# Out-projection left to the scheduler, every group of the up-projection with two token pairs

## The chip, the cores and the metric

The kernel runs on one core of one Trainium2 chip. The metric is the device time of one execution in microseconds (us): the median of several runs. Five kinds of work appear in the profile: TensorE matmuls (PE) and its weight loads (PEld), VectorE (DVE), ScalarE (ACT), GpSimd (POOL) and the DMA engines. SyncE (SP) and POOL issue the DMAs. Each engine takes its instructions in one order, fixed when the program is built.

## The reference

One step of a one-layer streaming encoder, for 2048 new tokens and 64 tokens of a running stream. After a mixer (a recurrent branch and an attention branch, added to `mixed`) comes a feed-forward block with a width-3 causal convolution over the tokens:

```python
x = x + mixed @ w_out                       # 1024 -> 1024
xn2 = rmsnorm(x, norm_ffn)
up = xn2 @ w_up                             # 1024 -> 5632
up_c = causal_dwconv(up, ...)               # three taps per channel
gate, val = split(up_c)
x = x + (silu(gate) * val) @ w_down         # 2816 -> 1024
y = rmsnorm(x, norm_final)
```

All is float32. The kernel splits each matmul operand into a high and a low part and adds three products (high by high, high by low, low by high).

## The kernel before

The 2112 tokens form three **pairs** of column blocks (`PAIRS`): pairs 0 and 1 have 2 x 304 columns each, pair 2 has 2 x 448. The kernel has four stages after one another: the mixer with its projections (stage 1, up to line 734), the out-projection (`wout`, lines 852 to 871), the up-projection (the loop over `plan`, lines 1408 to 1516) and the down-projection (the loop over `seq`, from line 1577).

**Order.** In stage 1 the tile framework's scheduler orders the instructions of each engine: it simulates the core and, among the instructions that are ready in its simulation, takes the one that stands first in the program. From line 739 on (`tc.manual_schedule()`) the order on each engine is the order in which the Python program states the instructions. So the interleaving of stages two to four is written out by hand: generators such as `mixes`, `xprep`, `xsums` and `xread` are driven a few pieces at a time between the matmuls (`drive`), and dictionaries `later` and `then` hold work that is due in a given step.

**Out-projection.** For each pair `i` and each of 8 row blocks `m`, two half weights (`weights[j]`) are multiplied with the pair's two blocks, 24 matmuls for each half weight. In pair 0 the weights come raw from `w_out` and are split (`wsplit`), and a POOL DMA stores the split form in `woS` (line 398); in pairs 1 and 2 `wload` (line 390) reads them back on SP, 512 KB each. Beside this run: loads of `mixS` and their splits into the operands of the next pair (`mixes`, lines 363 to 372), the residual (line 875) with its loads of `xT` (line 849) and stores of `x1S` (line 876) on POOL, and `xprep`, which prepares the operands of the up-projection of pairs 0 and 1 from `x1S` (loads on line 799, scaling on line 811, splits by `put2`). Three of pair 1's seven operands (`x1`, line 1389) are made in the up-projection's first four steps, in a region `FA` that takes the place of an out-projection operand region `RC`.

**Up-projection.** A group `g` is one of 22 row blocks of `w_up` with its partner 22 blocks on; groups `f` and `f + 11` follow one another. The two-by-two block product of a group with a pair is done with seven products in place of eight (Winograd's scheme), one product a step: `ORDER` names the seven token operands, `wops` makes the seven weight operands. A **lane** is one group with one pair; a product in a lane is 12 matmuls. `Lane.product` issues them, `Lane.after` takes the sums out of PSUM: in steps 0, 1, 2 and 6 on ACT (lines 1137, 1150), in steps 3, 4 and 5 on DVE (lines 1141, 1143, 1148). Then follow the convolution (`conv_a` on ACT, line 1122; `conv_b` on DVE, line 1128), the gate (lines 1153, 1162) and sums that are stored in `hS`.

`steps` gives the order: 20 groups with pairs 0 and 1 together (two lanes that share a weight, 140 steps); then groups 10 and 21 with pair 0 alone and after that with pair 1 alone (28 steps with one lane); then all groups with pair 2, two groups at a time (77 steps). With pair 0 alone done, `give(0)` frees all seven operands of pair 0 at once, and `xread` starts to read pair 2's operands into the space: 28 reads of 224 KB from `xS`, each rounded on ACT and subtracted on DVE, with 5 buffers. `give(1)` frees pair 1 when its last step is done.

**Weights.** A weight operand is a combination of raw blocks (DVE, `comb`, line 934), rounded to its high part (ACT, line 205, in `split2`) and subtracted to the low part (DVE, line 206, a step later, through the list `plow`). The first time (`fresh`) four of seven are stored in `wuS` for pair 2. `prepare` does this in the step's middle, after the products are issued and ahead of `Lane.after`; there are 4 weight slots. Groups 10 and 21 get theirs from `wsums`, which makes them in halves beside the first steps, with two slots `wx`; their one-lane steps read them from `wuS` (line 930), and split three of seven again, for either pair.

**Beside the up-projection.** `fill` drives one piece a step: first `wsums` for groups 10 and 21, then `xsums`, which makes pair 2's operands in float32 and stores them in `xS` (96 pieces).

**Down-projection.** 33 steps for each of seven products; beside them `side` does residuals, squares, the last norm (`rms`, line 752, whose sum over channels is a matmul) and the outputs (line 1571), two pieces a step from product 4 on. The last product ends with pair 0, `(i, p) == (6, 0)`, in 33 small steps.

Of the kernel before, what the change touches and what calls it, by code (L numbers as in the profile page):

```python
# [7 lines left out]
F32 = mybir.dt.float32  # L8
# [6 lines left out]
P = 128  # L15
# [3 lines left out]
NF = 22  # L19
# [107 lines left out]
def kernel(ctx: ExitStack, tc: tile.TileContext, xT, w_in, w_out, w_up, w_dn, gw, pk,  # L127
# [609 lines left out]

    es2 = ExitStack()
    es2.enter_context(tc.manual_schedule())
# [38 lines left out]
    def give(p):  # L778
        for region, part in xparts.pop(p):
            region.taken.remove(part)  # L780
# [132 lines left out]
    plow = []  # L913

    def wops(g, fresh):
# [3 lines left out]
        def parts(src):  # L919
            t = wh.tile([P, 2, 4 * P], F32R, name="wh")  # L920
            plow.append(split2(t[:, 0], t[:, 1], src))
            return t

        def kept_s(i, src):
            t = wh.tile([P, 2, 4 * P], F32R, name="wh")
            if fresh:
                low = split2(t[:, 0], t[:, 1], src())
                plow.append(lambda: (low(), nc.gpsimd.dma_start(wuS[g, i], t.bitcast(F32))))
            else:
                nc.sync.dma_start(t.bitcast(F32), wuS[g, i])  # L930
# [20 lines left out]

    def wsums(g, pool, out):

        for h in range(2):
            def draw(o, name):
                t = pool.tile([P, 2 * P], F32, name=name)
                c = 4 * P * (o[1] == "2") + h * 2 * P
                nc.sync.dma_start(t, w_up[g + NF * (o[0] == "2")][:, c:c + 2 * P])
                return t

            low = []

            def keep(i, src):
                t = out.tile([P, 2, 2 * P], F32R, name="wx", bufs=2)
                f = split2(t[:, 0], t[:, 1], src)
                low.append(lambda: (f(), nc.gpsimd.dma_start(wuS[g, i][:, :, h * 2 * P:(h + 1) * 2 * P],
                                                             t.bitcast(F32))))

            a, b, c, d = draw("11", "wa"), draw("21", "wb"), draw("22", "wc"), draw("12", "wd")
            for _ in range(4):  # L970
                yield
            nc.vector.tensor_tensor(a, a, b, op=ALU.subtract)
            keep(0, a)
            yield
            low.pop(0)()
            nc.vector.tensor_tensor(a, c, a, op=ALU.subtract)
            keep(1, a)
            yield
            low.pop(0)()
            nc.vector.tensor_tensor(b, b, c, op=ALU.add)  # L980
            keep(2, b)
            yield
            low.pop(0)()
# [796 lines left out]
```

## Time and profile before

| what | value |
|---|---|
| runs shown | 3041.38 us median of 3 (3038.78 to 3042.38) |
| profiled execution, its own time | 3043.69 us |
| its span, first to last instruction | 3041.9 us |
| matmuls | 17640, PE busy 2886.8 us |
| DVE busy | 2064.7 us (68%) |
| ACT busy | 1541.4 us (51%) |
| POOL busy | 450.5 us (15%) |
| HBM traffic | 195 GB/s over the span |

Busy time of PE overstates its work, because matmuls overlap one another. A better measure is the distance from the start of one matmul to the start of the next: where nothing is waited for it is constant, and a stretch's length less its matmuls times that distance is what the stretch loses. A window counts the instructions that touch it, so it counts about two matmuls too many.

### The profile page before, as it was taken

The numbers are of one execution on the slowest core, as the hardware profiler recorded it, in microseconds if no ns is written. First come the engines' busy times: TensorE is split into PE (matmuls) and PEld (weight loads), VectorE is DVE, ScalarE is ACT, GpSimd is POOL, SyncE is SP. The second block draws the span as 40 slices with busy tenths as digits, with TensorE's granted clock in tenths as the row PEclk, the third lists the DMA queues.
The fourth block names the chain that finished last, engine by engine and source line by source line (L and its number), as shares of the span: only waits on it lengthen the run. The fifth ranks groups of instructions, "written<-read, shape, count | busy, mean of one in ns | idle before, by whom it ended". The sixth has DMA issues, their size and how long they took to land. (4 is left out here: it accounts for less than half of the span.)

```text
span 3041.9 us, 48860 instructions
## 1 busy us (share of the span) xinstructions
PE 2886.8 (95%) x17640; PEld 2764.9 (91%) x17640; DVE 2064.7 (68%) x4048; ACT 1541.4 (51%) x3426; POOL 450.5 (15%) x655
## 2 busy tenths in 40 slices
PE   8999999999999999998797999999899999999998
PEld 7989889999998999997797999999799998999997
DVE  5388783477775378774656888888666656656676
ACT  4577772476672476673323555554544444433432
POOL 3232112000000000004120333333000101000001
PEclk9999999999999999998898999999999999999999
DMA  7776547534336544328774656566866666977563
GB/s 246 262 237 196 181 153 243 178 128 136 124 118 205 184 137 144 119 84 287 241 237 146 216 210 219 205 220 220 314 209 215 208 218 190 273 219 217 157 213 118
DMA packets 324499, 595.37 MB, mean 196 GB/s; under 512 B 37168, under 2 KB 224544, under 8 KB 307360
## 3 DMA queue, kind: packets, MB, share of 16 engines
q1 hardware_dynamic: 285728, 461.45, 47.4%
q0 software_dynamic: 38528, 130.79, 11.6%
q8 instruction: 139, 2.28, 0.3%
q14 instruction: 104, 0.85, 0.1%
HBM read 400.99 MB, written 191.64 MB: 195 GB/s over the span
## 5 line engine op out<-in xcount | busy, mean ns | idle before, releaser
L230 PE MATMUL mm<-xh,whl 128*128 128x320 f32 (+2 forms) x2112 | 692.3, 328 | 10.0 <-ACT xh L200 5.2
L231 PE MATMUL mm<-xl,whl 128*128 128x320 f32 (+2 forms) x2112 | 689.4, 327 | 7.6 <-POOL xl L201 3.8
L232 PE MATMUL mm<-xh,whl 128*128 128x320 f32 (+2 forms) x2112 | 688.2, 326 | 1.4 <-POOL whl L201 1.4
L205 ACT ACTIVATE RE<-FW 128x512 fp32r<-128x512 f32 (+3 forms) x556 | 296.8, 554 | 475.1 <-DVE FW L934 114.9
L230 PEld LDWEIGHTS mm<-xh,whl 128*128 128x128 f32 x2112 | 403.5, 191 | 17.0 <-ACT xh L200 8.1
L231 PEld LDWEIGHTS mm<-xl,whl 128*128 128x128 f32 x2112 | 403.1, 191 | 15.9 <-POOL xl L201 6.4
L232 PEld LDWEIGHTS mm<-xh,whl 128*128 128x128 f32 x2112 | 402.6, 191 | 2.4 <-POOL whl L201 1.7
L206 DVE TENSOR_TENSOR RE<-FW,RE 128x512 fp32r<-128x512 f32 (+3 forms) x556 | 319.9, 596 | 104.4 <-ACT RE L205 103.5
L1128 DVE SCALAR_TENSOR_TENSOR FA<-FA,pkt 128x608 f32<-128x608 f32 (+1 forms) x264 | 245.9, 951 | 71.6 <-ACT FA L1122 67.0
L1092 PE MATMUL mf<-RA,RE 128*128 128x304 f32 (+1 forms) x608 | 201.4, 331 | 10.6 <-ACT FW L1137 8.2
L1591 PE MATMUL mf<-RE 128*128 128x304 f32 (+2 forms) x616 | 198.9, 323 | 7.1 <-ACT RE L205 4.7
L1094 PE MATMUL mf<-RA,RE 128*128 128x304 f32 (+1 forms) x608 | 199.6, 328 | 4.8 <-DVE RE L206 4.8
L1592 PE MATMUL mf<-RE 128*128 128x304 f32 (+2 forms) x616 | 199.0, 323 | 0.2 <-DVE RE L206 0.2
L1093 PE MATMUL mf<-RA,RE 128*128 128x304 f32 (+1 forms) x608 | 199.0, 327 | 0.0
L1593 PE MATMUL mf<-RE 128*128 128x304 f32 (+2 forms) x616 | 197.8, 321 | 0.0
L1122 ACT ACTIVATE FA<-FA,pkt 128x608 f32<-128x608 f32 (+1 forms) x132 | 128.4, 973 | 110.4 <-DVE FA L1143 104.2
L1092 PE MATMUL mf<-RE 128*128 128x304 f32 (+1 forms) x488 | 159.9, 328 | 12.9 <-ACT RE L205 9.6
L1093 PE MATMUL mf<-RE 128*128 128x304 f32 (+1 forms) x488 | 159.9, 328 | 1.6 <-DVE RE L206 1.6
L1094 PE MATMUL mf<-RE 128*128 128x304 f32 (+1 forms) x488 | 159.9, 328 | 0.0
L201 POOL TENSOR_TENSOR gl<-gr,gh 128x256 fp32r<-128x256 f32 x24 | 22.4, 932 | 789.0 <-ACT gh L200 789.0
L1092 PEld LDWEIGHTS mf<-RA,RE 128*128 128x128 f32 x608 | 115.3, 190 | 18.9 <-ACT FW L1137 11.8
L1092 PE MATMUL mm<-RE 128*128 128x304 f32 (+1 forms) x392 | 125.4, 320 | 7.2 <-ACT FW L1137 4.4
(331 smaller groups left out, 7132.4 us busy)
## 6 DMA issues: line engine op xcount, KB each, us to landing
whl<-wiS SPq DMA_DIRECT2D x88, 1024.0 KB, 5.1
RE<-wuS SPq DMA_DIRECT2D x104, 512.0 KB, 4.5
wiS<-whl SPq DMA_DIRECT2D x44, 1024.0 KB, 4.8
wuS<-RE POOLq DMA_DIRECT2D x80, 512.0 KB, 3.8
FW<-in_w_up_dram SPq DMA_DIRECT2D x158, 256.0 KB, 5.1
hS<-FA POOLq DMA_DIRECT2D x154, 152.0 KB, 3.9
FW<-hS SPq DMA_DIRECT2D x154, 152.0 KB, 3.5
FW<-in_w_in_dram SPq DMA_DIRECT2D x44, 512.0 KB, 5.8
```

What stands on the lines that cost most here:

```text
L205: nc.scalar.activation(hi, src, AF.Copy)
L206: return lambda: nc.vector.tensor_tensor(lo, src, hi.bitcast(F32), op=ALU.subtract)
L230: nc.tensor.matmul(ps[:, :n], wh[:, c], xh[:, k, :n], start=first, stop=False)
L231: nc.tensor.matmul(ps[:, :n], wh[:, c], xl[:, k, :n], start=False, stop=False)
L232: nc.tensor.matmul(ps[:, :n], wl[:, c], xh[:, k, :n], start=False, stop=last)
L1092: nc.tensor.matmul(ps[:, :n], w[:, 0, c], x[:, k, 0], start=first, stop=False, **more)
L1093: nc.tensor.matmul(ps[:, :n], w[:, 0, c], x[:, k, 1], start=False, stop=False, **more)
L1094: nc.tensor.matmul(ps[:, :n], w[:, 1, c], x[:, k, 0], start=False, stop=last, **more)
L1128: nc.vector.scalar_tensor_tensor(uc, G[:, j:j + self.cols], col("fw", 44 * j + m), uc, op0=ALU.mult, op1=ALU.add)
L1591: nc.tensor.matmul(ps[m][:, cs], w[:, 0, c], t[:, 0], start=k == 0, stop=False)
L1592: nc.tensor.matmul(ps[m][:, cs], w[:, 0, c], t[:, 1], start=False, stop=False)
L1593: nc.tensor.matmul(ps[m][:, cs], w[:, 1, c], t[:, 0], start=False, stop=k == 10)
```

## The change

All 22 groups run with pairs 0 and 1 together (154 steps), so the one-lane steps, `wsums` and the slots `wx` go, and there are 5 weight slots. In the last group's seven steps (`last` is its first step) `give(p, u)` frees operand `u` of pairs 0 and 1 as soon as its product has been issued, and `xread` puts pair 2's operands there, up to three reads a step, with 3 buffers in the first steps and 5 after; `free` says in which step room for one more operand of pair 2 is open. `xsums` advances in three steps of four. The manual order is entered behind the out-projection, at the up-projection's loop; the out-projection, with the first three weights and with `xprep` as far as it runs there, is ordered by the scheduler. The rounding of weights (`phigh`) is held back until `rounded()`, behind `Lane.after`. In the down-projection the last pair drives one side piece a step in place of two.

```diff
--- before.py
+++ after.py
@@ -734,9 +734,7 @@
     es1.close()
 
 
-
     es2 = ExitStack()
-    es2.enter_context(tc.manual_schedule())
     pff = es2.enter_context(tc.tile_pool(name="pff", bufs=5, space=PSUM))
     bank = [0]
 
@@ -775,9 +773,9 @@
         xparts.setdefault(p, []).append((region, part))
         xops[p, o] = region.view(part, [P, 4, 2, n])
 
-    def give(p):
-        for region, part in xparts.pop(p):
-            region.taken.remove(part)
+    def give(p, q):
+        region, part = xparts[p][q]
+        region.taken.remove(part)
 
     def put2(p, o, k, src):
         return split2(xops[p, o][:, k, 0], xops[p, o][:, k, 1], src)
@@ -910,7 +908,11 @@
         nc.sync.dma_start(t, w_up[m][:, c:c + 4 * P])
         return t
 
-    plow = []
+    phigh, plow = [], []
+
+    def rounded():
+        while phigh:
+            phigh.pop(0)()
 
     def wops(g, fresh):
 
@@ -918,14 +920,18 @@
 
         def parts(src):
             t = wh.tile([P, 2, 4 * P], F32R, name="wh")
-            plow.append(split2(t[:, 0], t[:, 1], src))
+            phigh.append(lambda: plow.append(split2(t[:, 0], t[:, 1], src)))
             return t
+
+        def keep(i, t, src):
+            low = split2(t[:, 0], t[:, 1], src)
+            plow.append(lambda: (low(), nc.gpsimd.dma_start(wuS[g, i], t.bitcast(F32))))
 
         def kept_s(i, src):
             t = wh.tile([P, 2, 4 * P], F32R, name="wh")
             if fresh:
-                low = split2(t[:, 0], t[:, 1], src())
-                plow.append(lambda: (low(), nc.gpsimd.dma_start(wuS[g, i], t.bitcast(F32))))
+                src = src()
+                phigh.append(lambda: keep(i, t, src))
             else:
                 nc.sync.dma_start(t.bitcast(F32), wuS[g, i])
             return t
@@ -948,44 +954,6 @@
         yield kept_s(2, lambda: comb("21", "21", "22", ALU.add))
         yield parts(r["12"])
         yield kept_s(3, lambda: comb("12", "12", "11", ALU.subtract))
-
-    def wsums(g, pool, out):
...
     def xsums(p, pool, rpool, width):
 
@@ -1027,15 +995,15 @@
                 for _ in range(2):
                     yield
 
-    def xread(p, names, pool):
+    def xread(p, names, pools):
 
         n, raw = PAIRS[p][0][1], []
         todo = [(o, k) for o in names for k in range(4)]
         low = None
         for j, (o, k) in enumerate(todo):
-            while len(raw) < min(j + 4, len(todo)):
+            while len(raw) < min(j + len(pools[-1].slots["xs"]) - 1, len(todo)):
                 oo, kk = todo[len(raw)]
-                raw.append(pool.tile([P, n], F32, name="xs", bufs=5))
+                raw.append(pools[-1].tile([P, n], F32, name="xs"))
                 nc.sync.dma_start(raw[-1], xS[ORDER.index(oo), kk])
             if k == 0:
                 operand(p, o)
@@ -1067,11 +1035,10 @@
     class Lane:
 
 
-        def __init__(self, g, p, lanes):
-
-            self.g, self.p, self.steps = g, p, (1, 2, 3, 3) if p == 2 else (1, 4, 3, 4)
-            if len(lanes) == 1:
-                self.steps = (1, 2, 2, 2) if p == 1 and g == 21 else (1, 5, 5, 6)
+        def __init__(self, g, p):
+
+            self.g, self.p = g, p
+            self.steps = (1, 2, 3, 3, 4) if p == 2 else (1, 2, 2, 2, 2) if g == 21 else (1, 4, 3, 4, 5)
             (self.t0, self.n), (self.t1, _) = PAIRS[p]
             self.cols = 2 * self.n + (2 if self.t1 + self.n > TP else 0)
 
@@ -1178,7 +1145,7 @@
             def sums_c():
                 nc.vector.tensor_tensor(h[:, :n], h[:, :n], self.e[:, :n], op=ALU.subtract)
 
-            s, a, b, c = self.steps
+            s, a, b, c, d = self.steps
             if g < 11:
                 at(s, lambda: store("11", h[:, :n]))
                 at(a, sums_a)
@@ -1188,15 +1155,12 @@
                 at(b, sums_b)
                 at(c, sums_c)
                 at(c, lambda: (store("T2", self.e[:, :n]), store("T3", self.e[:, n:])))
-                at(c if p == 1 and s == a - 1 == c - 1 else c + 1, lambda: store("T4", h[:, :n]))
+                at(d, lambda: store("T4", h[:, :n]))
 
     def steps():
-        forder = [f + o for f in range(11) for o in (0, 11)]
-        for f in forder[:20]:
-            yield [(f, 0), (f, 1)], True
-        for p in (0, 1):
-            for f in forder[20:]:
-                yield [(f, p)], False
+        for f in range(11):
+            for g in (f, f + 11):
+                yield [(g, 0), (g, 1)], True
         for f in range(11):
             yield [(f, 2), (f + 11, 2)], False
 
@@ -1358,9 +1322,8 @@
                 tp.close()
                 wr.reserve("wr", 4 * P, 4)
                 wh.close()
-                wh.reserve("wh", 8 * P, 4)
+                wh.reserve("wh", 8 * P, 5)
                 wh.turn["wh"] = 2
-                wh.reserve("wx", 4 * P, 2)
                 prime(0)
                 prime(0)
             work = wout(i, m, besides if i == 0 or m > 0 else lambda: drive(side, pace[0] if i == 1 else 0))
@@ -1369,6 +1332,7 @@
             if i == 2 and m == 7:
                 for made in (0, 1, 2):
                     prepare(made)
+                    rounded()
                 made = 3
         residual(i, 7, work)
         drive(side, 99)
@@ -1396,41 +1360,39 @@
 
     lane_sums(BS)
     up["c"].reserve("G", 2 * BS + 2, 3)
+
+    es2.enter_context(tc.manual_schedule())
     fill, x2, raw2 = [], [], [0]
 
 
-    live, extra = [], [10, 21]
+    live = []
 
     def fits(i):
         return sum(len({g for g, _ in plan[q][0]}) for q in range(i, min(made + 1, len(plan)))) <= len(wh.slots["wh"])
 
+
+    last, free = 21 * 7, (1, 1, 2, 2, 4, 4, 5)
     px = rx = None
     for i, (lanes, fresh, u) in enumerate(plan):
         if u == 0:
-            live = [Lane(g, p, lanes) for g, p in lanes]
-            if lanes == [(10, 0)]:
-
-                assert not extra
-                wh.close("wx")
-                wh.extend("wh", 8 * P, 1)
-            if lanes == [(10, 1)]:
-
-                drive(fill, 999)
-                px.close()
-                rx.close()
-                give(0)
+            live = [Lane(g, p) for g, p in lanes]
+            if i == last:
+                xs = [Pool(FW, FA)]
+                xs[0].reserve("xs", BM, 3)
+                x2 = [xread(2, ORDER, xs)]
+            if i == last + 7:
                 RD.close()
                 FP = Region(tc, "FP", 9728, F32, "right")
-                px = Pool(FP)
-                x2 = [xread(2, ORDER, px)]
-            if lanes == [(0, 2), (11, 2)]:
-                assert raw2[0] <= 17
-                drive(x2, 17 - raw2[0])
-                give(1)
+                xs.append(Pool(FP))
+                xs[1].reserve("xs", BM, 5)
                 up["s"].close()
                 up["s"] = Pool(FW)
-                lane_sums(BM)
+                for name in ("p1", "p7"):
+                    up["s"].reserve(name, BM, 2)
                 wh.extend("wh", 8 * P, 4)
+        if i == last + 9:
+            xs[0].close()
+            up["s"].reserve("V", BM, 2)
         clock[0] = i
         for f in later.pop(i, ()):
             f()
@@ -1443,6 +1405,9 @@
             up["u"].reserve("uc", 2 * BM + 2, 4)
         for lane in live:
             lane.product(u, ready[i, lane.g])
+        if last <= i < last + 7:
+            give(0, u)
+            give(1, u)
         while made < len(plan) + 1 and fits(i):
             prepare(made)
             made += 1
@@ -1450,6 +1415,7 @@
             f()
         for lane in live:
             lane.after(u)
+        rounded()
         if i < 4:
             drive(x1, 5)
             if i == 0:
@@ -1472,25 +1438,24 @@
             lane_sums(BS)
             up["h"].reserve("hp", 2 * BS, 4)
             px, rx = Pool(FW), Pool(FA)
-        if i > 6 and not fill:
-            if extra:
-                px.close()
-                fill = [wsums(extra.pop(0), px, wh)]
-            elif px.regions[0] is FW and lanes != [(10, 1)] and lanes[0][1] == 0 and not raw2[0]:
-                px.close()
-                fill = [xsums(2, px, rx, BM // 2)]
-                raw2[0] = 1
-        drive(fill, 1)
-        if x2:
-            if lanes[0][1] == 1:
-                for _ in range(2):
-                    if raw2[0] < 17:
-                        drive(x2, 1)
-                        raw2[0] += 1
-            else:
-                drive(x2, 99 if u == 3 else 3)
-                if u == 3:
-                    px.close()
+        if i == 7:
+            fill = [xsums(2, px, rx, BM // 2)]
+        if i % 4 != 3:
+            drive(fill, 1)
+        if i == last - 1:
+            drive(fill, 999)
+            px.close()
+            rx.close()
+        if last < i < last + 11:
+
+            q = sum(i - last >= f for f in free)
+            for _ in range(3):
+                if raw2[0] < 4 * q:
+                    drive(x2, 1)
+                    raw2[0] += 1
+            if i == last + 10:
+                drive(x2, 99)
+                xs[1].close()
         if lanes[0] == (0, 2) and u == 4:
             up["h"].reserve("hp", 2 * BM, 2)
 
@@ -1514,7 +1479,8 @@
             dloads(0, 10)
             tparts(0)
             tparts(1)
-    give(2)
+    for q in range(7):
+        give(2, q)
     wh.extend("wh", 8 * P, 6)
     dr.extend("hh", 2 * BM, 5)
 
@@ -1605,7 +1571,7 @@
                 tparts(len(seq) - 36 + k)
             if k < 6:
                 raw[6, 0, k - 2] = dtoken("T4", 0, k - 2)
-        drive(side, 3 if R is None else 1 if i < 4 else 2)
+        drive(side, 3 if R is None else 1 if i < 4 or (i, p) == (6, 0) else 2)
         if j == 8:
 
             drive(side, 99)
```

## The prediction on record

> **What bounds the kernel now.** I read the page first (busy times, slices), then the windows by stage, then for each stage with a loss the waits of PE, and behind these the waits of the engine that PE waited for.
>
> ```profile
> span 3041.9 us, 48860 instructions
> PE 2886.8 (95%) x17640; PEld 2764.9 (91%) x17640; DVE 2064.7 (68%) x4048; ACT 1541.4 (51%) x3426; POOL 450.5 (15%) x655
> PE   8999999999999999998797999999899999999998
> ```
>
> PE is busy nearly throughout; slices 20, 22 and 29 show 7, 7 and 8. The question is what PE loses where. The windows give it (us, then busy time and count for PE, PEld, DVE, ACT, POOL; granted clock, DMA share, GB/s):
>
> ```profile
> 700.00:1300.00 600.00, 589.05 (x3628) 572.52 (x3627) 413.18 (x979) 362.26 (x802) 15.17 (x17) 0.99 0.45 146
> 1956.00:1996.00 40.00, 40.00 (x289) 40.00 (x288) 33.48 (x61) 18.96 (x46) 13.91 (x26) 1.00 0.64 214
> 2190.00:2540.00 350.00, 350.00 (x1695) 317.92 (x1694) 210.24 (x308) 156.25 (x388) 37.60 (x70) 1.00 0.66 220
> 1371.77:1521.82 150.05, 120.99 (x773) 118.18 (x773) 82.62 (x173) 48.42 (x107) 44.38 (x76) 0.88 0.79 268
> 1521.82:1602.01 80.19, 80.19 (x390) 72.85 (x389) 45.99 (x86) 18.79 (x38) 20.16 (x37) 1.00 0.69 229
> 1602.01:1647.64 45.63, 27.89 (x149) 25.33 (x148) 32.04 (x55) 14.74 (x34) 3.77 (x7) 0.74 0.48 156
> 1647.64:2110.26 462.62, 453.81 (x3218) 449.01 (x3217) 393.72 (x683) 238.67 (x568) 150.25 (x276) 1.00 0.60 209
> 2110.26:2175.39 65.13, 50.62 (x338) 48.60 (x337) 43.47 (x74) 33.65 (x77) 10.69 (x20) 0.97 0.86 289
> 2998.00:3020.40 22.40, 17.84 (x123) 15.88 (x121) 20.84 (x36) 8.39 (x20) 4.56 (x9) 1.00 0.32 111
> ```
>
> Rows two and three hold no loss: two edge matmuls taken off, a 304-column matmul starts every 40/287 = 0.1394 us, a 448-column one every 350/1693 = 0.2067 us. A two-lane step (24) is 3.35 us, a one-lane step 1.67 us, a pair 2 step 4.96 us. With the counts from the code:
>
> - Out-projection, pairs 0 and 1 (row four): 768 matmuls are 107.1 us of 150.05; lost 43.0. Pair 2 (row five): 384 are 79.4 of 80.19; lost 0.8.
> - First six up-projection steps (row six): 144 are 20.1 of 45.63; lost 25.6.
> - The other two-lane steps (row seven): 3216 are 448.3 of 462.62; lost 14.3.
> - One-lane steps (row eight): 336 are 46.8 of 65.13; lost 18.3.
> - Pair 2 (row three): nothing.
>
> About 102 us are lost in a quarter of the span, and the change touches nearly each of these places. The matmuls stay the same in number and shape: one-lane steps load weights for each matmul just as two-lane steps do.
>
> **Part 1: the out-projection in the scheduler's order.** PE's waits from 1371.77 to 1602.01, and some of SP's there (total, times, longest):
>
> ```profile
> PE mf L863 <- DMA RE<-woS: 11.5, 3, 7.7
> PE mm L863 <- DMA RE<-woS: 6.8, 1, 6.8
> PE mf L865 <- DVE RA L206: 4.4, 3, 1.9
> PE mm L865 <- DVE RA L206: 4.0, 2, 2.7
> PE mm L863 <- ACT RA L205: 3.6, 1, 3.6
> PE mf L863 <- ACT RA L205: 2.4, 1, 2.4
> ...
> SPq L363 <- DVE RE L206: 24.5, 6, 7.4
> SPq L390 <- PE mm L865: 21.7, 6, 5.0
> SPq L799 <- DVE FW L819: 19.7, 4, 9.0
> ...
> RE<-woS SPq DMA_DIRECT2D x32, 512.0 KB, 5.7
> ```
>
> PE waits 32.7 us in all; the other 11 of 43.8 are matmuls at a low clock after a wait (clock 0.88). Of the waits 18.3 us are late `woS` weights. They land 5.7 us after issue, and with five slots each is allowed some three steps, 10 us; late they are because SP stands at an `x1S` load (line 799) or a `mixS` load (line 363) whose buffer isn't free yet, with the `woS` load behind it. An order made by readiness puts the ready load first. So the 18.3 us go, and of the low clock their share, 11 x 18.3/32.7 = 6.2: 24 us. The RA waits (14.4) I leave: the first 6.3 are the split of pair 0 at the stage's start, which is data, and the others hang on `woS` stores in POOL's order and on transfers. What is late next are these. Ends: 38 gained (all but the first 6), or 50 lost (first rival). That readiness order can work here is row one: stage 1 is in that order, and in 600 us PE is idle for 11. But it moves 146 GB/s, and the out-projection 268.
>
> **Part 2: the first six steps.** Nothing gained.
>
> ```profile
> PE mf L1092 <- ACT RE L205: 9.6, 2, 6.9
> PE mf L1094 <- DVE RE L206: 4.1, 1, 4.1
> ...
> DVE FA L811 <- DMA FA<-x1S: 9.1, 4, 3.7
> ```
>
> PE waits for operand T1 of pair 1, four rounds of load, scale, split, subtract and split, which can't start before the out-projection's last matmul frees RC. The order is stated there before and after. The fifth slot adds a weight to step 0 (one rounding, one subtraction, 1.3 us by the durations in part 3) and takes it from a later step: 3 us either way.
>
> **Part 3: roundings last.** In row seven DVE is busy for 85%, ACT for 52%. PE's waits there, ACT's longest, and one case from the timeline:
>
> ```profile
> PE mf L1092 <- ACT FW L1137: 7.6, 10, 1.4
> ...
> ACT RE L205 <- DVE FW L934: 111.8, 51, 6.2
> ...
> 1808.46 0.68 DVE L934 TENSOR_TENSOR FW<-FW 128x512 f32<-128x512 f32 x1
> 1809.17 0.63 ACT L205 ACTIVATE RE<-FW 128x512 fp32r<-128x512 f32 x1 [1.88 <-DVE FW L934]
> 1809.70 0.72 ACT L1137 ACTIVATE FW<-mf 128x304 f32<-128x304 f32 x2
> 1810.16 0.41 PE L1092 MATMUL mf<-RA,RE 128*128 128x304 f32 x1 [1.40 <-ACT FW L1137]
> ```
>
> ACT's rounding (line 205) stands ahead of the copies out of PSUM and waits for DVE's `comb`, which queues behind convolution and `xsums`; the copies come late, and PE's next product into that bank waits. With the copies first this wait goes. Against it: the rounding now ends up to two copies and itself, 0.72 + 0.63 = 1.35 us, behind a step's end, and DVE's low part early in the next step queues `comb` and convolution behind it. DVE has 0.15 x 3.35 = 0.5 us free a step, so in some steps it will run late. The weights are needed four steps on, which hides that. Of 14.3 us I take 10; ends 0 and 14. `wsums` gone and `xsums` in three steps of four lie on DVE beside PE: no term of their own.
>
> **Part 4: no one-lane steps, operand by operand.** Waits from 2110.26 to 2178, and the reads of pair 2 there:
>
> ```profile
> PE mm L1092 <- ACT FW L1137: 7.8, 3, 3.4
> PE mf L1092 <- ACT FW L1137: 3.8, 2, 3.3
> ...
> ACT RA L205 <- DMA FP<-xS: 9.8, 6, 3.7
> ...
> L205 ACT ACTIVATE RA<-FP 128x448 fp32r<-128x448 f32 x16 | 8.8, 572 | 9.9 <-DMA FP<-xS 9.8
> FP<-xS SPq DMA_DIRECT2D x28, 224.0 KB, 5.1
> ```
>
> ACT stands 9.8 us in the one-lane steps for reads of `xS`, with PSUM copies queued behind: two reads a 1.67 us step, with five buffers. Those steps go, and their 18.3 us with them. But 18 reads now fall into six two-lane steps, three in 3.35 us, with three buffers and two reads ahead. A buffer's turn is landing (5.1; the `mixS` loads of that size took 4.7), rounding 0.57, subtraction 0.62: 6.3 us. Three buffers pass three reads in that time, where a step has 3.35. If ACT is held the whole of it, a step is 6.3: five steps (the first three reads are ahead) lose 15 us. Steps 3, 4 and 5 leave PSUM on DVE, not on ACT, the buffers' turn shortens where fewer bytes move (row eight 289 GB/s, row seven 209), and PE is a step ahead: I take 8, between 0 and 15. So 10 us gained; ends 3 and 18. Freeing operand by operand costs nothing: a space is written only after copies that waited for the same products.
>
> **Part 5: one side piece a step in the last pair.**
>
> ```profile
> PE mm L1592 <- DVE RE L206: 3.4, 4, 2.0
> PE mm L752 <- DVE FD L1558: 2.1, 2, 1.2
> PE mf L752 <- DVE FD L1558: 1.1, 1, 1.1
> ```
>
> In the last row of the windows DVE is busy for 20.84 of 22.40 us: two outputs of a side piece each stand ahead of the token's low part. Half as many a step halve PE's 6.6 us: 3 gained. One or two output pieces go behind the last matmul, about 0.5 each; ends -1 and 6.
>
> **Sum.** 24 + 0 + 10 + 10 + 3 = 47 us. The profiled execution took 3043.7 us (span 3041.9, 1.8 around it): 2996.7. It stood 2.3 over the median of the runs, so 2994.
>
> **Rivals.**
>
> *The transfers bind the out-projection.* Pairs 0 and 1 move 150.05 us x 268 GB/s = 40.2 MB. The densest stage row is 289 GB/s at a DMA share of 0.86; at that rate 40.2 MB take 139 us, whatever the order, and part 1 gains 11 in place of 24: 3007. For it: a share of 0.79 already. Against: pair 2 runs without loss at 229 GB/s. The Trainium skill, "DMA: Bandwidth & Descriptors", section Specifications, puts the HBM limit of a core at about 358 GB/s; by it the bytes would take an estimated 112 us and not bind, and part 1 could give up to 38. No row here shows such a rate over a stage.
>
> *The order does not change to the better.* The scheduler goes by the program's order among what is ready; if its simulated transfers are quicker than the real ones, it finds SP never blocked and repeats the stated order. Part 1 gives 0: 3018.
>
> *Slower.* The same fault in a worse form: by modelled times it issues `woS` loads one step ahead of use. A landing of 5.7 us against a step of 3.35 is 2.35 late, with the low clock after it (11/32.7 of a wait) 3.1; in pair 2 5.7 - 4.96 = 0.7, 1.0 with the clock. 16 steps of each: 66 us, less the 24.5 of woS waits and their clock that are there now, is 41 lost. With the other parts' 23 gained: 3041 + 18 = 3059. It decides from 23 us lost on. Every queue that the loads pass on SP bears on it; against it is row one.
>
> *Buffers.* ACT held the whole time by three buffers, 15 us: part 4 gains 3, and all else as forecast 3001.
>
> **How the numbers follow.** 0.2% (6 us) is about what a measurement here can tell from no change. Forecast, the buffers' case with it: 0.48. Transfers bind: 0.20. Order not better: 0.15. Slower: 0.12. An out-projection that loses about what the rest gains: 0.05. So faster 0.83, same 0.05, slower 0.12. Low end: parts 1, 3, 4 and 5 at their better ends add 14 + 4 + 8 + 3, part 2 3: 2994 - 32 = 2962. High end: the order rival (3018) with part 4 at its worse end (7) and part 3 at 0 (10) is 3035; above it lie the last two cases, 0.17.
>
> **What would show it.** Right: from the first out-projection matmul to the first of the up-projection about 206 us in place of 230; the six first steps at 43 to 49; the group "ACT L205 <- DVE L934" near nothing, and PE waits for L1137 in the two-lane steps under 3 us; no `wx`; in the last group's seven steps some 8 us of waits on PSUM copies behind `FW<-xS`; pair 2 without loss. Wrong: an out-projection of 230 us or more, `RE<-woS` still among PE's waits, DVE later in the two-lane steps with PE waiting for line 1141 or 1143, or a new gap where the manual order begins.

## The result, and the profile after

The changed kernel took 3001.53 us in the median (four runs, 3000.28 to 3006.32), the kernel before 3041.88 (four runs, 3038.78 to 3049.98): a ratio of 0.9866, with the interval 0.9844 to 0.9888. The forecast was 2994, in a range of 2962 to 3035. The profiled execution took 3006.32 us (span 3004.6), 37.3 less in its span than the one before; the medians differ by 40.4.

Three lines of the page, then the windows by stage (us, then busy time and count for PE, PEld, DVE, ACT, POOL; granted clock, DMA share, GB/s). Each window begins and ends with the first matmul of a stage.

```profile
span 3004.6 us, 48626 instructions
PE 2870.3 (96%) x17640; PEld 2755.8 (92%) x17640; DVE 2059.1 (69%) x4026; ACT 1544.0 (51%) x3412; POOL 444.9 (15%) x647
PE   8989999999998999998897999999899999999997
```

```profile
1373.00:1499.27 126.27, 114.01 (x772) 112.51 (x773) 78.37 (x169) 49.97 (x106) 43.03 (x74) 0.92 0.90 310
1499.27:1579.47 80.20, 80.20 (x390) 72.85 (x389) 48.28 (x94) 19.62 (x40) 20.21 (x37) 1.00 0.72 245
1579.47:1628.88 49.41, 27.72 (x150) 25.30 (x148) 31.70 (x55) 15.15 (x35) 3.78 (x7) 0.72 0.41 133
1628.88:2077.33 448.45, 448.45 (x3218) 448.45 (x3217) 384.15 (x654) 238.50 (x553) 140.54 (x262) 1.00 0.58 203
2077.33:2125.82 48.49, 47.09 (x338) 46.87 (x337) 37.61 (x64) 27.58 (x61) 10.22 (x20) 1.00 0.62 205
2125.82:2178.20 52.38, 42.44 (x194) 38.01 (x193) 35.45 (x58) 27.79 (x70) 6.42 (x12) 0.90 0.79 283
2960.87:2987.60 26.73, 25.64 (x204) 24.53 (x202) 22.05 (x39) 7.23 (x18) 6.55 (x13) 1.00 0.25 88
2987.60:3004.60 17.00, 2.02 (x7) 1.12 (x6) 9.99 (x28) 1.87 (x6) 2.58 (x5) 0.57 0.42 134
```

The counts of matmuls are those of before, so stage can be set against stage. A **half-step** is the 12 matmuls of one lane: 1.67 us with pairs 0 and 1, of which there are 308 in either kernel, and 2.48 us with pair 2. Loss is length less matmuls times their spacing, 0.1394 and 0.2067 us, as in the prediction.

| stretch | before | after | gained | forecast |
|---|---|---|---|---|
| out-projection, first matmul to first of the up-projection | 230.2 | 206.5 | 23.7 | 24 |
| first six steps, length | 45.6 | 49.4 | -3.8 | 0 |
| other steps up to half-step 280 (all two-lane), loss | 14.2 | 0.0 | 14.2 | 10 |
| half-steps 280 to 308 (one-lane before), loss | 18.3 | 1.6 | 16.7 | } 10 |
| first 16 half-steps of pair 2 (308 to 324), loss | 1.0 | 12.7 | -11.7 | } |
| down-projection up to the last matmul of its products (its last 33 steps: 32.5, 26.7) | 470.1 | 463.7 | 6.4 | } 3 |
| behind that matmul (the last norm with its own matmuls, outputs) | 10.1 | 17.0 | -6.9 | } |

With 1.2 us lost ahead of the out-projection and 0.1 in the rest of pair 2 the rows give 37.3, the difference of the spans. The two largest terms are as forecast or better. Two stretches that were to lose nothing now lose: the start of pair 2 and the tail.

What PE waits for after, in the out-projection (first fence), the first six steps (second) and around the start of pair 2 (third): total, times, longest.

```profile
PE mf L750 <- DVE FW L882: 11.1, 1, 11.1
PE mm L861 <- ACT RA L205: 4.0, 1, 4.0
PE mm L863 <- DVE RA L206: 1.2, 1, 1.2
```

```profile
PE mf L1059 <- ACT RE L205: 12.7, 2, 6.9
PE mf L1059 <- ACT FA L1104: 5.8, 1, 5.8
PE mf L1060 <- DVE RE L206: 3.1, 2, 2.5
```

```profile
PE mf L1061 <- DVE RE L206: 7.9, 1, 7.9
PE mf L1059 <- issue: 1.8, 1, 1.8
PE mf L1059 <- DVE FA L1110: 1.4, 1, 1.4
```

`RE<-woS` is gone from the out-projection's list. By the two traces five of the 32 stored weights landed 0.2 us or less ahead of their first matmul in the kernel before, and none less than 1.5 us ahead after; the shortest time from a load's issue to that matmul grew from 4.2 to 7.1 us. In its place stands one wait of 11.1 us of the norm's matmul (line 750) for a sum of squares. The timeline shows what that sum stood behind: SP's queue, then ACT's.

```profile
1430.15 20.14 SPq L363 DMA_DIRECT2D FW<-mixS  x12
...
1433.49 0.58 ACT L205 ACTIVATE RE<-FW 128x448 fp32r<-128x448 f32 x1 [8.21 <-DMA FW<-mixS]
1438.86 0.58 ACT L205 ACTIVATE RC<-FW 128x448 fp32r<-128x448 f32 x1 [3.32 <-DMA FW<-mixS]
```

Twelve `mixS` loads hold SP for 20 us, since they wait for buffers; ACT's roundings wait for the loads, with the squares of the residual behind them.

### The profile page after: what moved, and what is told of

Its sections match the earlier page's. It is cut to its first block, busy times and chain, and to the rows that moved or that the text cites. A ratio compares the mean times of both kernels' runs of the same rounds, so it can differ in the third digit from the quotient of the medians.

```text
span 3004.6 us, 48626 instructions
## 1 busy us (share of the span) xinstructions
PE 2870.3 (96%) x17640; PEld 2755.8 (92%) x17640; DVE 2059.1 (69%) x4026; ACT 1544.0 (51%) x3412; POOL 444.9 (15%) x647
## 5 line engine op out<-in xcount | busy, mean ns | idle before, releaser
L205 ACT ACTIVATE RE<-FW 128x512 fp32r<-128x512 f32 (+2 forms) x544 | 290.2, 559 | 418.4 <-DVE FW L940 101.7
L206 DVE TENSOR_TENSOR RE<-FW,RE 128x512 fp32r<-128x512 f32 (+2 forms) x544 | 315.7, 601 | 173.8 <-ACT RE L205 168.4
L1061 PE MATMUL mf<-RA,RE 128*128 128x304 f32 (+1 forms) x620 | 204.2, 329 | 7.9 <-DVE RE L206 7.9
L1059 PE MATMUL mf<-RA,RE 128*128 128x304 f32 (+1 forms) x620 | 204.2, 329 | 5.8 <-ACT FA L1104 5.8
L1060 PE MATMUL mf<-RA,RE 128*128 128x304 f32 (+1 forms) x620 | 203.4, 328 | 0.0
L1059 PE MATMUL mf<-RE 128*128 128x304 f32 (+1 forms) x480 | 157.0, 327 | 14.8 <-ACT RE L205 12.7
L1060 PE MATMUL mf<-RE 128*128 128x304 f32 (+1 forms) x480 | 156.7, 326 | 3.1 <-DVE RE L206 3.1
L1061 PE MATMUL mf<-RE 128*128 128x304 f32 (+1 forms) x480 | 156.5, 326 | 0.0
L510 ACT ACTIVATE pr<-S,nm 128x256 f32<-128x256 f32 (+1 forms) x272 | 122.9, 465 | 12.6 <-DVE nm L506 12.4
```

The source lines that it names most:

```text
L205: nc.scalar.activation(hi, src, AF.Copy)
L206: return lambda: nc.vector.tensor_tensor(lo, src, hi.bitcast(F32), op=ALU.subtract)
L1059: nc.tensor.matmul(ps[:, :n], w[:, 0, c], x[:, k, 0], start=first, stop=False, **more)
L1060: nc.tensor.matmul(ps[:, :n], w[:, 0, c], x[:, k, 1], start=False, stop=False, **more)
L1061: nc.tensor.matmul(ps[:, :n], w[:, 1, c], x[:, k, 0], start=False, stop=last, **more)
```

## The experiments

The sizes below are those of the table, each read from that run's own trace. "B" is the kernel before, "A" the changed one; each ratio is to runs of B made beside that experiment's. "Two-lane loss" is the loss of the table's third row, "one-lane loss" that of its fourth.

**1. The order alone** (B, with the manual order entered behind the out-projection).

```diff
     es2 = ExitStack()
-    es2.enter_context(tc.manual_schedule())
...
     up["c"].reserve("G", 2 * BS + 2, 3)
+    es2.enter_context(tc.manual_schedule())
```

> The kernel before, with the stated order entered behind the out-projection and nothing else changed. Theory (a ready weight load passes the loads that wait on SP, so the woS waits of PE go): the out-projection takes 207 us in place of 230 (from its first matmul to the up-projection's first), PE waits for woS are gone, the time is 3018 us; the two-lane steps still lose 14 us and the one-lane steps 18. Rival (the out-projection got faster in the changed kernel because of the fifth weight slot or because roundings come last, and the order does nothing): 230 us there and 3041 in all. If the wait for the norm's matmul that stands in the changed kernel belongs to the scheduler's order, it is here too, 10 us or more.

Measured 3010.36 us, 0.9899 of B (0.9883 to 0.9916). The out-projection takes 205.9 in place of 230.2. First six steps 45.2, two-lane loss 13.1, one-lane loss 18.8: all nearly as in B. The norm's wait is there as well, 11.5 us, so it comes with the scheduler's order. The other 7 us of the profile's gain lie in pair 2 (338.5 us in place of 345.6), where the order was not changed; they are told of at the end.

**2. The order taken back** (A, with the order stated by hand from line 739 on again).

> The changed kernel with the stated order entered where it was, ahead of the out-projection. Theory: the out-projection is back at 230 us with PE waiting 18 us for woS, and the time at 3025 us; all later stages as in the changed kernel. Rival (the scheduler's order gained elsewhere, at the seam to stage 1 or in the first six steps): the out-projection moves by less than 12 us and the rest stands elsewhere.

Measured 3031.55 us, 0.9970 of B (0.9956 to 0.9983). The out-projection is back at 232.9, and PE's waits in it (below) have the stored weights at their head again. Added to B or taken from A, the order is worth 24 to 26 us, and only there.

```profile
PE mf L862 <- DMA RE<-woS: 13.4, 4, 7.4
```

**3. The norm one row block later** (A; `norms(i - 1)` is called behind row block 1, not 0, and the side work that goes with it starts one block later).

> The changed kernel with the norm of a pair, whose sum is a matmul, stated one row block later in the next pair's out-projection (and xprep started one row block later). Theory (PE, which runs ahead now, reaches that matmul before DVE has the sum of squares, and stands 11 us): that wait falls under 3 us, the out-projection from 206.5 to about 194 us, the time to 2990 us. Rival (PE would be late there for another reason, the mixS loads that SP and ACT stand for): the wait moves to another instruction and the stage stays at 203 us or more.

Measured 3009.32 us, 0.9896 of B (0.9876 to 0.9917); out-projection 207.0 in place of 206.5. PE's waits in it:

```profile
PE mf L750 <- DVE FW L882: 4.4, 1, 4.4
PE mm L861 <- ACT RA L205: 3.6, 1, 3.6
PE mf L861 <- DMA RE<-woS: 2.0, 2, 1.1
PE mf L861 <- DVE RA L206: 1.9, 1, 1.9
```

The norm's wait falls from 11.1 to 4.4, and waits for stored weights come back, with one for a split operand. So moving the norm does not shorten the stretch; PE seems to wait for whatever is first needed of what stands behind the queue of `mixS` loads; that is argued, not shown. What a larger set of buffers for these would give wasn't tried.

**4. Roundings last, alone** (B with `rounded()` and its list `phigh`; nothing else).

> The kernel before, with the roundings of the weights held back behind the copies out of PSUM and nothing else changed. Theory (ACT's rounding waits for DVE with the copies queued behind it): the 14.3 us that the two-lane steps lose fall to under 1, PE has no wait for the copy on ACT there, the time is 3028 us. Rival (the two-lane steps were freed by xsums in three steps of four and by wsums gone, which unload DVE): they still lose 10 us or more and the time is 3038 or above.

Measured 3028.70 us, 0.9959 of B (0.9944 to 0.9973). The two-lane loss falls from 14.2 to 4.9, the one-lane loss from 18.3 to 15.2. Of PE's waits for PSUM copies in the two-lane steps, 7.6 us in the row of B, 2.9 are left (line 1100 is B's 1092, 1145 its 1137). The loss is neither the under 1 of the theory nor the 10 of the rival; where it stays is told under run 7.

```profile
PE mf L1100 <- ACT FW L1145: 2.9, 3, 1.0
```

**5. Roundings first again** (A).

```diff
             prepare(made)
+            rounded()
             made += 1
```

> The changed kernel with the roundings where they were, ahead of the copies out of PSUM. Theory: the two-lane steps lose 10 to 16 us again, on PE waits for the copy on ACT, and the time is 3012 to 3016 us; the first six steps, which grew by 3.7 us, get 1 to 4 back if the later roundings were what they grew by. Rival (xsums at three quarters of the rate is what freed the steps): under 4 us lost there, time within 4 us of the changed kernel's.

Measured 3000.83 us, 0.9864 of B (0.9847 to 0.9880). The two-lane loss stays at 0.0. The idle time of ACT's rounding grows, and PE does not feel it. The groups of line 205 in the two-lane steps, first of A, then of this run (busy, mean ns, idle before and what ended it):

```profile
L205 ACT ACTIVATE RE<-FW 128x512 fp32r<-128x512 f32 x133 | 81.5, 627 | 103.6 <-DVE FW L940 88.3 <-issue 7.1 <-PE mm L1061 4.0
```

```profile
L205 ACT ACTIVATE RE<-FW 128x512 fp32r<-128x512 f32 x134 | 82.5, 628 | 140.9 <-DVE FW L940 125.7 <-issue 8.1 <-PE mf L1061 3.5
```

So roundings last take away two thirds of the loss in B, and nothing in A. Something else in A is enough by itself.

**6 and 7. What it is.** Both start from run 5, with roundings first. In the one the sums of pair 2 are driven in every step again, as in B; in the other there are four weight slots again up to pair 2 (then five are added, nine in all as ever).

```diff
-        if i % 4 != 3:
-            drive(fill, 1)
+        drive(fill, 1)
```

> The changed kernel with the roundings first again (as in the run that lost nothing by that), and the sums of pair 2 driven in every step as before the change, not in three of four; still no wsums, still five slots. Theory (rate of the side work): the loss in the two-lane steps comes back in part, 3 to 10 us of the 14.2, since DVE's comb again queues behind the side work and ACT's rounding stands ahead of the copies. Rival (fifth slot): a weight prepared a step earlier decouples it, and the loss stays under 1 us.

```diff
-                wh.reserve("wh", 8 * P, 5)
+                wh.reserve("wh", 8 * P, 4)
...
-                wh.extend("wh", 8 * P, 4)
+                wh.extend("wh", 8 * P, 5)
```

> The changed kernel with the roundings first again and four weight slots in the two-lane steps as before the change (five are added for pair 2, so that it has nine as ever); sums in three steps of four. Theory (rate of the side work): two-lane steps lose under 1 us still. Rival (fifth slot): 3 to 10 us come back. Apart from that: if the fifth slot is what made the first six steps longer (45.6 to 49.4), they are 45 to 46 here; if not, 49 to 50.

One run each: 2996.03 us (sums in every step) and 3001.76 (four slots). With the sums in every step the two-lane loss is 0.0: with five slots the rate of the side work does not matter, and that theory falls. With four slots it is 4.7 and, more, half-steps 280 to 324 lose 14.5 + 6.2 = 20.7, where run 5 loses 0.6 + 12.8. So the fifth slot is the remedy that works in A: a weight made a step earlier is not late when its rounding is. It does not account for all of B's 14.2, which are two losses. Up to step 45 B makes `wsums` beside its steps:

| two-lane loss | steps 6 to 45 | steps 46 to 139 |
|---|---|---|
| B | 6.6 | 7.6 |
| run 4: B with roundings last | 4.9 | 0.0 |
| run 7: A with four slots and roundings first | 0.1 | 4.6 |
| A, runs 5 and 6 | 0.0 | 0.0 |

The later loss goes by either remedy, roundings last or the fifth slot. The earlier one mostly stays with roundings last, and is gone where `wsums` are gone, with four slots too; `wsums` were not put back by themselves, so that they are its cause is likely and not shown. Nor was the slower pace of the sums tried alone with four slots: it may be what lies between 7.6 and 4.6.

The slot has a price: with four, the first six steps take 45.2 us, as in all kernels with four slots (45.1 to 45.6), and with five 49.1 to 51.2. How it lengthens these steps was not followed. Run 7's waits there, to be set against A's 12.7, 5.8 and 3.1 above:

```profile
PE mf L1059 <- ACT RE L205: 9.1, 2, 6.4
PE mf L1061 <- DVE RE L206: 4.4, 1, 4.4
PE mf L1059 <- ACT FA L1104: 2.2, 1, 2.2
PE mf L1060 <- DVE RE L206: 1.6, 1, 1.6
```

**8. Two reads a step in the last group, not three** (A).

```diff
-            for _ in range(3):
+            for _ in range(2 if i < last + 7 else 3):
```

> The changed kernel with two reads of pair 2 a step in place of three in the last group's six steps after its first; three a step after that. Theory (three reads outrun three buffers: ACT stands for loads with copies behind it, and DVE with the low part of the next weight behind ACT): ACT's waits for xS between the last group and pair 2 fall from 20 us to under 8, the loss at the change to pair 2 (14.9 us from the last two steps of the group to the third of pair 2) to under 6, the time to 2993 us. Rival (ACT and DVE have too much to do there, however the reads arrive): the rounding and subtraction only move to later steps, the loss stays over 11 us.

Measured 2996.54 us, 0.9858 of B (0.9836 to 0.9880). Half-steps 280 to 308 lose nothing, but 308 to 324 lose 13.4 (A: 12.7): 4.3 of it at half-step 308 and 7.2 at 318, where reads put off now fall. The pace of the reads moves the loss and hardly lessens it.

**9. The work without the loads** (A; the loads of pair 2's operands are left out after the first three, up to pair 2; their roundings and subtractions still run, on what lies in the buffers).

> The changed kernel with the loads left out of the reads of pair 2 in the last group (all but the first three): rounding and subtraction run on what stands in the three buffers, so a part of pair 2's operands holds other data. Theory (the landing of the loads is the cost): ACT has no wait for xS in those steps and the loss at the change to pair 2 falls from 14.9 us to under 4. Rival (the work of rounding and subtracting 18 reads beside six two-lane steps is the cost): over 9 us are still lost.

One run, 2980.56 us. Half-steps 280 to 308 lose 0.0 and 308 to 324 1.6, in place of 12.7. (Of the rest that it is below A, 6.6 us are pair 2's pace, told of at the end.) The window of pair 2's start and PE's waits around it (line 1062 is A's 1061):

```profile
2114.00:2156.00 42.00, 39.90 (x201) 36.77 (x200) 32.72 (x55) 23.98 (x60) 5.34 (x10) 1.00 0.81 288
```

```profile
PE mf L1062 <- DVE RE L206: 2.1, 1, 2.1
```

So the roundings and subtractions cost nothing; waiting for the loads does. This window moves 288 GB/s nearly without loss, A's moves 283 with its 12.7 lost, so a mere limit on bytes in that window does not explain it. With a load left out both its landing and its wait on SP for a buffer go; the run does not tell these apart.

**10. Low parts in every step** (A). How a load holds PE up is seen in A's timeline. ACT's readings of pair 2's operands (128x448), with the convolution (line 1089) among them, and then DVE. In the row at 2121.58 two roundings of weights (128x512) and one more reading are merged.

```profile
2115.79 0.58 ACT L205 ACTIVATE RA<-FW 128x448 fp32r<-128x448 f32 x1 [2.79 <-DMA FW<-xS]
2116.36 0.58 ACT L205 ACTIVATE RA<-FA 128x448 fp32r<-128x448 f32 x1
2116.91 0.58 ACT L205 ACTIVATE RA<-FW 128x448 fp32r<-128x448 f32 x1
2120.03 0.58 ACT L205 ACTIVATE RA<-FW 128x448 fp32r<-128x448 f32 x1 [2.54 <-DMA FW<-xS]
2121.10 0.58 ACT L205 ACTIVATE RE<-FA 128x448 fp32r<-128x448 f32 x1 [0.49 <-DMA FA<-xS]
2121.58 1.61 ACT L205 ACTIVATE RE<-FW 128x512 fp32r<-128x512 f32 x3
2123.90 0.58 ACT L205 ACTIVATE RE<-FW 128x448 fp32r<-128x448 f32 x1 [0.71 <-DMA FW<-xS]
2126.36 0.58 ACT L205 ACTIVATE RE<-FA 128x448 fp32r<-128x448 f32 x1 [1.88 <-DMA FA<-xS]
...
2126.94 0.88 ACT L1089 ACTIVATE FA<-FA,pkt 128x608 f32<-128x608 f32 x1
...
2128.93 1.03 ACT L205 ACTIVATE RA<-FW 128x448 fp32r<-128x448 f32 x2
...
2127.85 3.39 DVE L1095 SCALAR_TENSOR_TENSOR FA<-FA,pkt 128x608 f32<-128x608 f32 x4 [1.94 <-ACT FA L1089]
...
2133.52 1.29 DVE L206 TENSOR_TENSOR RE<-FW,RE 128x512 fp32r<-128x512 f32 x2
```

Ten readings from 2115.79 to 2129.4, 13.6 us from the first to the last of them: 1.5 each, 4.5 for three, where a step has 3.35. The loads themselves land in some 3 us (over the last group and the start of pair 2):

```profile
FW<-xS SPq DMA_DIRECT2D x13, 224.0 KB, 3.0
```

The convolution on ACT stands behind the readings that wait, DVE's part of it (3.39 us) behind that, and the low parts of pair 2's first weights (2133.52) behind that. PE waits for these. They come so late also because low parts are taken only together with the next weight, which has no slot free in the step before pair 2.

```diff
+        while plow:
+            plow.pop(0)()
         while made < len(plan) + 1 and fits(i):
             prepare(made)
```

> The changed kernel with one thing more: low parts of weights that are still outstanding are taken in every step, ahead of the look for a further weight to prepare; before, they were taken only together with the next weight, which in the step before pair 2 does not come, since no slot is free. Theory (late low parts): the 9.9 us lost at the first pair 2 step, with 7.9 of PE waiting for a subtraction into RE, are this; they fall under 3, the time by some 8 to 3.5 thousandths less, 2993 to 2998 us. Rival (landing of loads): DVE and ACT are held there by the last xS loads, and a subtraction asked for earlier stands in the same queue: the loss stays at 8 to 13, the time within 5 us of the changed kernel's.

Measured 3001.23 us, 0.9876 of B (0.9853 to 0.9898). Half-steps 308 to 324 lose 16.1 (A: 12.7). Run 3, whose edit lies in another stage, loses 16.1 there too, so 3 us between two executions tell nothing here. The low parts are nearly on time (half-step 308 loses 1.7 in place of A's 9.9), and PE stands for a stored weight one half-step on; its load stands on SP (second fence, line 936) behind reads that wait for a buffer:

```profile
PE mf L1059 <- DMA RE<-wuS: 7.3, 1, 7.3
```

```profile
2120.40 0.86 SPq L1007 DMA_DIRECT2D FW<-xS  x2
2127.69 0.32 SPq L1007 DMA_DIRECT2D FA<-xS  x1
...
2129.20 0.32 SPq L936 DMA_DIRECT2D RE<-wuS  x1
```

**11. Slots three steps earlier as well** (run 10; the four further slots are made at `last + 4`; and in the last output pair one and two side pieces by turns).

```diff
-                wh.extend("wh", 8 * P, 4)
+        if i == last + 4:
+            wh.extend("wh", 8 * P, 4)
...
-        drive(side, 3 if R is None else 1 if i < 4 or (i, p) == (6, 0) else 2)
+        drive(side, 3 if R is None else 1 if i < 4 or (i, p) == (6, 0) and j % 2 else 2)
```

> The changed kernel with the low parts taken in every step, with the four further weight slots of pair 2 made at the last group's fifth step (where two spaces of the operands used up have come free) in place of at the first pair 2 step, and with one and two side pieces by turns in the last output pair, in place of one. Theory (SP's order): in the run with the low parts alone the first stall went and PE then waited 7.3 us for a stored weight, loaded behind xS loads that wait on SP for a buffer; with slots three steps earlier these weights are asked for ahead of the held loads, so half-steps 308 to 324 lose under 5 us in place of 12.7 to 16.1; the side pieces shorten the tail from 17 to 12 or 14 and cost the last 33 steps 2 or 3; the time is 2983 to 2995 us. Rival (landing of the xS loads themselves, into three buffers, with PE or ACT waiting for operand T4 or T1): 10 us or more stay lost there, or move ahead into half-steps 296 to 308, and the time is within 5 us of the changed kernel's.

Measured 3009.43 us, 0.9895 of B (0.9879 to 0.9912). The loss at half-steps 308 to 324 is 16.1 again: the theory falls, the rival holds. The stored weights are there, and PE waits for a low part once more, behind a reading for which ACT stands 7.4 us, since the weights' loads now stand ahead of it on SP: its load lands 8.6 us after issue. The waits of PE and of ACT around the start of pair 2:

```profile
PE mf L1061 <- DVE RE L206: 9.0, 1, 9.0
PE mf L1059 <- ACT FW L1104: 2.9, 1, 2.9
...
ACT RE L205 <- DMA FW<-xS: 7.4, 1, 7.4
```

The last 33 steps and the tail take 36.1 + 10.3 = 46.4 us, where A takes 26.7 + 17.0 = 43.7: a miss as well.

**12. Two side pieces in the last pair again** (A).

```diff
-        drive(side, 3 if R is None else 1 if i < 4 or (i, p) == (6, 0) else 2)
+        drive(side, 3 if R is None else 1 if i < 4 else 2)
```

> The changed kernel with two side pieces a step in the last pair again. The profiles say that one piece a step took 6 us from the last product's matmuls and put 7 us behind the last matmul. Theory (work only moved from one side of the last matmul to the other): the last 33 steps take 32.6 us and the rest behind them 10.1 again, and the time is within 2 us of the changed kernel's 3001.5, rather 1 lower. Rival, the forecast's part 5: 3 us slower, 3004.5.

Measured 2998.20 us, 0.9860 of B (0.9840 to 0.9880). The last 33 steps take 32.3 and the tail 9.8, 42.1 in all: part 5 of the change moves some 6 us from the one to the other and gains nothing.

No run that does the whole work beats the changed kernel clearly. Sums in every step with roundings first (2996.03, one run), two reads a step (2996.54) and two side pieces (2998.20) are ahead of it by less than the intervals.

## Why the prediction was right

The sign and the largest term were right for the reason given. Of the forecast 47 us the profiles show 37.3; the terms differ from the forecast in both directions, so that the total is as near as it is partly by luck.

**Part 1 (24 forecast, 23.7 measured): right, to the microsecond by luck.** The order alone makes it, both ways (runs 1 and 2), and through the waits named: `RE<-woS` leaves PE's list. But the forecast left the other waits as they were: of the 14.4 us of RA waits 5.2 remain, and the norm's matmul, which it did not name, brings 11.1, behind SP's held `mixS` loads. These two nearly cancel.

**Part 2 (0, with 3 either way; measured -3.8): mis-sized.** That the fifth slot "adds a weight to step 0" and "takes it from a later step" does not net out: run 7 shows the fifth slot to cost 4 us there.

**Part 3 (10; measured 14.2): right in size, wrong on what does it here.** Run 4 confirms the mechanism in the kernel before: 9.3 of 14.2. But run 5 shows that in the changed kernel it is worth nothing, since the fifth slot, which the prediction counted in part 2 alone, does the same work. Two steps failed. The prediction noted that the weights are "needed four steps on" and did not ask what a fifth does to a wait of a microsecond. And it gave the end of `wsums` "no term of their own"; as far as the runs tell that was wrong, for 6.6 of the 14.2 lie beside them and run 4 leaves 4.9 of these. That the group "ACT L205 <- DVE L934" would be "near nothing" was wrong too: 88.3 us of it are left in the two-lane steps, and cost nothing.

**Part 4 (10; measured 5.0): the cause right, mis-sized and misplaced.** The one-lane steps' 18.3 us go. The turn of three buffers was put at 6.3 us, with a landing of 5.1 in it; three readings took 4.5, with a landing of 3.0, against 3.35 a step. The loss was put at 8, in the last group's steps with "pair 2 without loss". It is 14.3, nearly all of it at the start of pair 2. The step that failed is where a late reading is felt: not by the PSUM copies behind it on ACT at once, but through ACT's convolution, DVE, and the low parts of the first weights of pair 2. Run 9 shows that the loads are the cause, not the work on them. Runs 8, 10 and 11 mend one link each, and the loss comes back at the next: 13.4, 17.1 and 17.3 from half-step 280 on. Whether more buffers or less other traffic would end it stays open.

**Part 5 (3; measured -0.5): wrong.** The step that failed is "One or two output pieces go behind the last matmul, about 0.5 each". By the traces 17 pieces of the output stand there in A and 8 in B, and a second norm with its two matmuls. The tail grows by 6.9 us: a slower generator leaves all that it has not reached, and behind the last matmul it runs with nothing beside it.

**The rivals.** *The transfers bind*: refuted. The out-projection of pairs 0 and 1 moved 310 GB/s over 126 us, where the rival took 289 as the most. For 20 us in it the rate was 393, at a DMA share of 1.03 (a transfer counts where it starts, so a share can pass 1), and PE was busy throughout:

```profile
1394.70:1414.70 20.00, 20.00 (x146) 20.00 (x146) 10.07 (x22) 7.18 (x16) 7.22 (x12) 1.00 1.03 393
```

The Trainium skill, "DMA: Bandwidth & Descriptors", section Specifications, puts the limit at about 358 GB/s; this stretch lies above it, and the measurement decides.

*The order does not change to the better*: refuted by runs 1 and 2. *Slower*: did not come; `RE<-woS` is gone from PE's waits. Whether the scheduler reckons with quicker transfers than the real ones no run shows. *Buffers* came near in its number, 14.3 lost where the rival had 15, but not by its mechanism: the last group's steps, where it put the loss, lose 1.6.

## What to carry to other kernels

A loss with several sufficient remedies is credited to none of them by a change that brings two: add each alone, and take each away alone, before a cause is named. And a loss over a long stage may be two: set it apart where the work beside it changes. Where transfers wait for buffers on an in-order queue, ask of every engine that handles them what stands behind, link by link up to PE; mending one link moved the loss here and did not lessen it. Work slowed beside the last matmuls is not saved but put behind them, where it has no cover.

## What the runs showed of the hardware

A matmul of 448 columns starts after the one before at one of two distances, with the same code and a granted clock of 1.00 in both. The same 280 us of pair 2, first in A, then in run 8:

```profile
2200.00:2480.00 280.00, 280.00 (x1357) 254.28 (x1356) 167.98 (x243) 122.03 (x307) 30.18 (x56) 1.00 0.64 215
```

```profile
2200.00:2480.00 280.00, 280.00 (x1383) 259.54 (x1382) 169.18 (x244) 126.67 (x320) 30.18 (x56) 1.00 0.64 215
```

With two edge matmuls taken off, 280/1355 = 0.2066 us against 280/1381 = 0.2027, 2%: over the rest of pair 2, from half-step 324 on, it is 345.1 to 345.8 us in B, A and runs 5, 11 and 12, and 338.4 to 339.8 in all the others. In A it changed within one execution: half-steps 313 to 318 take 2.43 us each, those from 321 on 2.48, with a stall of PE in half-step 319 between them. In the part on the time before, the distance was called constant where nothing is waited for; that holds only between such changes. What sets the distance was not found. It makes 7 us between two executions, more than most of the edits above, and speaks for comparing kernels stage by stage. B and A both ran at the slower pace there, so the first table holds nothing of it.
